# A gated attention block: row sums of squares from x by rows, the last two groups scaled in one pass, and smaller staging

## The chip, the cores and the metric

The kernel runs on one core of one Trainium2 chip. The metric is the device time of one execution in microseconds (us). TensorE is called PE in the profile (PEld is its loading of weights), VectorE DVE, ScalarE ACT, GpSimd POOL, and SyncE, which issues the DMAs here, SP.

## The reference

One layer of a hybrid attention block on x of 2048 x 1024 in float32: an RMS norm, one wide projection, a banded attention (branch A), a sparse attention whose keys are picked by a small index (branch B), a gated merge, an output projection and a second RMS norm.

```python
def rms_norm(x, g):
    y = x * lax.rsqrt(jnp.mean(x * x, axis=-1, keepdims=True) + EPS)
    return y * g
...
xn = rms_norm(h, norm_gain)
proj = xn @ w_in
qa, ka, va, ga, qb, kb, vb, gb, iq, ik, iw, za, zb = jnp.split(proj, offsets, axis=-1)
ya = chunked_relpos_attention(qa, ka, va, rel_bias) * jax.nn.silu(ga)
qb, kb, iq, ik = (partial_rope(z) for z in (qb, kb, iq, ik))
yb = dsa_sparse_attention(qb, kb, vb, iq, ik, iw) * jax.nn.silu(gb)
merged = sigmoid(za + b_merge[0]) * (ya @ w_branch_a) + sigmoid(zb + b_merge[1]) * (yb @ w_branch_b)
h = x + merged @ w_out
out = rms_norm(h, final_norm_gain)
```

The sparse attention scores all earlier keys with relu(iq . ik) weighted by iw, keeps the best 256 per query and attends to these alone.

## The kernel before, in words

**Precision.** Every matmul operand is held as two float32r parts, a rounded high part and the rest, and a product is three matmuls (`mm3`, line 192): high x high, high x low, low x high. A chain is 8 slices k of the model width times 3, that is 24 matmuls into one accumulator of 128 x 512. So each operand needs a split: ScalarE copies the high part, and VectorE or GpSimd subtracts it.

**Order of the work.** The instructions of each engine run in the order in which a list scheduler put them when the program was built; it walks the program in its written order and simulates the engines, so that an instruction whose inputs and buffers are ready can go ahead of one written earlier. On the chip each engine, and SP's queue of DMAs, then goes strictly in that order. A tile with a tag rotates over `bufs` buffers; a new tile waits until the last user of the buffer is done.

**The start (lines 212 to 365).** x is worked on in four groups of 512 rows, in the order 2, 3, 0, 1 (`order`), from `xT`, which holds x transposed (the model width on the partitions). For each group i there are three chains m = 0, 1, 2 (`chain`, line 273) with the weights of the index queries, keys and weights (`load_w`, line 236, staged through tile `wst` of three buffers).
- `split_u` (243) splits x times the norm's gain (`gcol`), not yet divided by the root of its mean square, into xh and xl. There are two slots of xh and xl; groups 2 and 0 share one, 3 and 1 the other.
- `squares` (247): ScalarE squares the eight slices two at a time, GpSimd adds them up. `root_columns` (256): four matmuls with a vector of ones turn the sum into one column per 128 rows; VectorE makes the reciprocal square root in small steps (`rsqrt`, 133), GpSimd spreads it into `rb`. `root_rows` (265): four transposes and a ScalarE copy make of it a row that all partitions hold, `roots_[g]`.
- `evac_i` (281) empties an accumulator: times the roots (286), for m = 0 the rotation with the table `cs` (289 to 293), the split (296, 297), and stores to the scratch tensors iqD, kB and the tile ikT (303 to 308), 24 DMAs a group. `weights_t` (310) transposes the index weights.
- Five accumulators rotate over the 12 chains; two of them (tags acc0 and acc1 of pool `psp`) are also the first two of the main projection.
- `norm` (317) takes groups 0 and 1 a second time: VectorE multiplies x by the roots (322), and x is split again (`split_x`, 206), now scaled. These xh and xl are what the main projection reads first.

**The main projection (line 1144 on).** 20 units of 256 columns (`UNITS`), each for two groups at a time; `prep` (172) loads a unit's weights in pieces of two k through tile `wst` (186), ScalarE copies (188), GpSimd subtracts (189). The first unit's `prep(0)` is written in the start (358); its buffer is the one that x32, the tile with x of the groups 2 and 0, lies in. Between the chains the index logits (`logits`, 408) and the search for the best 256 (`search`, 446) are interleaved by a virtual clock. Halfway, groups 2 and 3 are split again, scaled (`norm_again`, 1133), and the units run once more. When the search is done, `open_early` (699) closes its memory and the attention begins beside the last units of the projection.

**The attention.** For each pair of heads the sums of the softmax are inverted, spread by GpSimd into `rb` (891) or `rbb` (969), transposed and multiplied with the gate (`finish`, 887, and `b_unit`, 959 to 977). Both tiles have the tag `ty`, one buffer, which is also that of the tile `ty` or `tyb`, through which one half of the head's output passes (876, 963).

Of the kernel before, what the change touches and what calls it, by code (L numbers as in the profile page):

```python
# [8 lines left out]
F32 = mybir.dt.float32  # L9
# [12 lines left out]
D = 1024  # L22
# [70 lines left out]
def block_kernel(ctx: ExitStack, tc: tile.TileContext, io, dbg=None):  # L93
# [35 lines left out]
    bm = consts.tile([128, 16], F32, name="bm")  # L129
    nc.sync.dma_start(bm, io["bm"])  # L130
    iw = consts.tile([128, NT, H], F32, name="iw")
# [25 lines left out]
    xpoolr = search_st.enter_context(pool("xTr", side="right"))  # L157
    ikT = xpoolr.tile([128, S], F32R, name="ikT")
# [11 lines left out]
    wcur = {}  # L170

    def prep(u, gate=None):
# [3 lines left out]
        if UNITS[u][0] == "va":  # L176
            st = wpool.tile([128, KT, 32], F32, name="wst", tag="wst", bufs=3)
# [3 lines left out]
        for c in range(2):  # L181
            for k in range(0, KT, 2):
                st = wpool.tile([128, 2, 128], F32, name="wst", tag="wst", bufs=3)
                if gate is not None:
                    nc.gpsimd.tensor_copy(st[:, 0, 0:1], gate)
                nc.sync.dma_start(st, io["wP"][u, c, :, k:k + 2, :])
                hi = wt[:, 0, k:k + 2, c * 128:(c + 1) * 128]
                nc.scalar.activation(hi, st, AF.Copy)  # L188
                nc.gpsimd.tensor_tensor(wt[:, 1, k:k + 2, c * 128:(c + 1) * 128], st, f32(hi), op=OP.subtract)  # L189
# [10 lines left out]
    ones = consts.tile([128, 1], F32, name="ones")  # L200
# [5 lines left out]
    def split_x(s, k, c, src):  # L206

        nc.scalar.activation(xh[s][:, k, c], src, AF.Copy, scale=gcol[:, k:k + 1])
        nc.vector.scalar_tensor_tensor(xl[s][:, k, c], src, gcol[:, k:k + 1], f32(xh[s][:, k, c]),
                                       op0=OP.mult, op1=OP.subtract)  # L210

    with ExitStack() as ph:
# [14 lines left out]
        rb, ra, rt, ssq = work[:, 2], work[:, 3], more[:, 2], more[:, 0:2]  # L227
# [8 lines left out]
        def load_w(m, k):  # L236
            st = wpool.tile([128, 2, 128], F32, name="wst", tag="wst", bufs=3)
# [5 lines left out]
        def split_u(i, c=all_):  # L243
            for k in range(KT):
                split_x(SLOT[order[i]], k, c, x32[i % 2][:, k, c])

        def squares(i):

            for k in range(0, KT, 2):
                sq = ssq if k == 0 else tk.tile([128, 2, 512], F32, name="sq", tag="gt", bufs=2)  # L250
                nc.scalar.activation(sq, x32[i % 2][:, k:k + 2], AF.Square)
                if k:
# [1059 lines left out]
```

## Time and profile before

| what | us |
|---|---|
| median of 3 runs (2237.25 to 2248.39) | 2240.68 |
| the profiled execution | 2252.72 |
| its span | 2250.9 |
| PE busy | 2099.3 |
| DVE busy | 1366.3 |
| ACT busy | 1231.5 |
| POOL busy | 950.8 |

The span is the time from the first to the last instruction of the profiled execution. Line numbers (L197) are those of the kernel before. A row of instructions gives line, engine, operation, output and inputs with their shapes, a count, the busy time and the mean duration in ns, and then the idle time before them and what ended it. A matmul's duration is longer than the distance between two of them, since they are pipelined; a rate is therefore taken from counts in a window.

### The profile page before, as it was taken

The numbers are of one execution on the slowest core, as the hardware profiler recorded it, in microseconds if no ns is written. First come the engines' busy times: TensorE is split into PE (matmuls) and PEld (weight loads), VectorE is DVE, ScalarE is ACT, GpSimd is POOL, SyncE is SP. The second block draws the span as 40 slices with busy tenths as digits, with TensorE's granted clock in tenths as the row PEclk, the third lists the DMA queues.
The fourth block names the chain that finished last, engine by engine and source line by source line (L and its number), as shares of the span: only waits on it lengthen the run. The fifth ranks groups of instructions, "written<-read, shape, count | busy, mean of one in ns | idle before, by whom it ended". The sixth has DMA issues, their size and how long they took to land. (4 is left out here: it accounts for less than half of the span.)

```text
span 2250.9 us, 34069 instructions
## 1 busy us (share of the span) xinstructions
PE 2099.3 (93%) x10890; PEld 1746.5 (78%) x10890; DVE 1366.3 (61%) x3296; ACT 1231.5 (55%) x2508; POOL 950.8 (42%) x1067
## 2 busy tenths in 40 slices
PE   6879999999999999999999888999999999999998
PEld 5667787878878888887977767788778877777786
DVE  7948978678778651012336657667676677664444
ACT  5435656556455552224437657667776678763221
POOL 5536456564463632223315453354333533333420
PEclk9989999999999999999999999999999999999999
DMA  5354344454444332337667553464345631144642
GB/s 195 96 154 125 111 150 130 143 184 132 160 153 138 131 100 100 107 103 235 177 203 228 151 180 114 151 215 153 94 124 167 200 115 38 53 127 131 217 158 85
DMA packets 254650, 322.29 MB, mean 143 GB/s; under 512 B 31744, under 2 KB 156032, under 8 KB 254336
## 3 DMA queue, kind: packets, MB, share of 16 engines
q1 hardware_dynamic: 254464, 320.05, 45.0%
q8 instruction: 87, 1.43, 0.3%
q14 instruction: 99, 0.81, 0.1%
HBM read 213.04 MB, written 105.87 MB: 142 GB/s over the span
## 5 line engine op out<-in xcount | busy, mean ns | idle before, releaser
L197 PE MATMUL acc<-xh,wt 128*128 128x512 f32 x2304 | 741.9, 397 | 6.6 <-ACT wt L188 4.5
L197 PEld LDWEIGHTS acc<-xh,wt 128*128 128x128 f32 x2304 | 434.5, 189 | 106.0 <-ACT wt L188 4.8
L197 PE MATMUL acc<-xl,wt 128*128 128x512 f32 x1152 | 455.0, 395 | 0.0
L189 POOL TENSOR_TENSOR wt<-wst,wt 128x256 fp32r<-128x256 f32 x304 | 241.0, 812 | 349.4 <-ACT wt L188 335.8
L773 POOL TENSOR_TENSOR ptl<-pf,pth 128x512 fp32r<-128x512 f32 (+1 forms) x144 | 179.0, 1243 | 241.9 <-ACT pf L769 204.1
L197 PEld LDWEIGHTS acc<-xl,wt 128*128 128x128 f32 x1152 | 218.0, 189 | 49.6
L776 DVE TENSOR_TENSOR ptl<-pt,pth 128x512 fp32r<-128x512 f32 (+1 forms) x288 | 188.3, 661 | 72.8 <-ACT pth L775 71.1
L436 DVE SCALAR_TENSOR_TENSOR sc<-r,iw,sc 128x512 f32<-128x512 f32 (+2 forms) x190 | 174.5, 937 | 78.5 <-POOL sc L434 47.7
L931 PE MATMUL s<-kBt,qsB 128*128 128x512 f32 (+3 forms) x640 | 192.0, 390 | 10.8 <-DVE mx L752 6.7
L775 ACT ACTIVATE pth<-pt 128x512 fp32r<-128x512 f32 (+1 forms) x288 | 161.6, 578 | 59.8 <-PE pt L948 36.8
L188 ACT ACTIVATE wt<-wst 128x256 fp32r<-128x256 f32 x304 | 115.3, 414 | 135.9 <-DMA wst<-wP 133.6
L428 ACT ACTIVATE r<-lg 128x512 f32<-128x512 f32 (+2 forms) x304 | 152.2, 545 | 67.6 <-DVE sc L436 26.9
L948 PE MATMUL pt<-ident,P 128*128 128x128 f32 x1088 | 171.2, 281 | 8.8 <-DVE sg L896 5.1
L934 ACT ACTIVATE P<-P,mx 128x128 f32<-128x128 f32 (+15 forms) x128 | 154.3, 1207 | 44.2 <-DVE mx L752 43.2
L956 PE MATMUL O<-pth,vBt 128*128 128x256 f32 x544 | 154.8, 300 | 16.7 <-ACT pth L775 7.9
L956 PE MATMUL O<-ptl,vBt 128*128 128x256 f32 x544 | 154.6, 308 | 4.5 <-POOL ptl L773 1.9
L948 PEld LDWEIGHTS pt<-ident,P 128*128 128x128 f32 x1088 | 130.9, 144 | 22.6 <-DVE sg L896 7.7
L752 DVE CUSTOM_DVE_ANT_0 P<-s,mk,mx 128x512 f32<-128x512 f32 (+2 forms) x192 | 125.3, 652 | 31.2 <-PE s L931 23.5
L994 POOL TENSOR_TENSOR dw<-dst,dw 128x512 fp32r<-128x512 f32 x64 | 82.9, 1295 | 129.9 <-ACT dw L993 117.2
L956 PEld LDWEIGHTS O<-pth,vBt 128*128 128x128 f32 x544 | 107.4, 197 | 30.6 <-ACT pth L775 11.5
L931 PEld LDWEIGHTS s<-kBt,qsB 128*128 128x128 f32 x640 | 103.7, 193 | 32.5 <-DVE mx L752 22.5
L956 PEld LDWEIGHTS O<-ptl,vBt 128*128 128x128 f32 x544 | 107.3, 197 | 17.8 <-DVE ptl L776 10.4
(227 smaller groups left out, 4261.9 us busy)
## 6 DMA issues: line engine op xcount, KB each, us to landing
wst<-wP SPq DMA_DIRECT2D x304, 128.0 KB
qs<-qA SPq DMA_DIRECT2D x128, 128.0 KB
kk<-kA SPq DMA_DIRECT2D x56, 256.0 KB
vs<-vA SPq DMA_DIRECT2D x56, 256.0 KB
bias<-biasD SPq DMA_DIRECT2D x32, 320.0 KB
sBD<-ef SPq DMA_DIRECT2D x32, 256.0 KB
sAD<-ef SPq DMA_DIRECT2D x32, 256.0 KB
qsB<-qB SPq DMA_DIRECT2D x16, 512.0 KB
```

The costliest lines, as they stand in the source:

```text
L189: nc.gpsimd.tensor_tensor(wt[:, 1, k:k + 2, c * 128:(c + 1) * 128], st, f32(hi), op=OP.subtract)
L197: nc.tensor.matmul(acc, a, b, start=(i == 0), stop=(i == n - 1))
L428: nc.scalar.activation(r[:, :w], lg[:, :w], AF.Relu)
L436: nc.vector.scalar_tensor_tensor(o_, r[:, :w], wv, o_, op0=OP.mult, op1=OP.add)
L752: nc.vector.tensor_tensor_reduce(dst, ps_, add, 1.0, FMAX if first else mx, OP.add, OP.min, accum_out=mx)
L773: nc.gpsimd.tensor_tensor(lo, pf, f32(hi), op=OP.subtract)
L775: nc.scalar.activation(hi, src, AF.Copy)
L776: nc.vector.tensor_tensor(lo, src, f32(hi), op=OP.subtract)
L931: nc.tensor.matmul(s_ps[:, :w], q[:, h, :], kBt[:, m, a:a + w], start=(m == 0), stop=(m == 1))
L934: nc.scalar.activation(P[:, e, :n], P[:, e, :n], AF.Exp, bias=mx[:, e:e + 1], scale=-1.0, accum_out=st["sum"][:, (u % 2) * 2 + e:(u % 2) * ...
L948: nc.tensor.transpose(pt[:, k, e, :], P[:, e, (kt + k) * 128:(kt + k + 1) * 128], ident)
L956: nc.tensor.matmul(o_, vBt[:, kt + k, :], src[:, k, :], start=(kt + k == 0 and n_ == 0), stop=(kt + k == b and n_ == 1), skip_group_check= ...
```

## The change

- Sums of squares: each group's 512 rows are loaded a second time by rows from `x` (four tiles of 128 x 1024, tag gt, two buffers), and ScalarE squares each and sums along the row. The squares of slices, GpSimd's adds and the matmuls with ones are gone.
- Groups 2 and 3 are treated as before (split unscaled, roots applied when the accumulator is emptied; for m = 0 the table cs is multiplied by the roots on GpSimd instead). Groups 0 and 1 are scaled and split in one pass ahead of their chains: VectorE multiplies by gain and root, ScalarE copies, GpSimd (two of eight slices VectorE) subtracts. Their accumulators are emptied without roots, and `norm` is gone. The roots of groups 0 and 1 are made together.
- The index weights have a staging tile of their own (`wis`, four buffers). The weights of the main projection are staged in pieces of four k through three buffers while the search's memory is open, and in pieces of two through two buffers before and after that.
- `rb` and `rbb` have a buffer of their own (pool `wz`). `bm`, `iw`, `ones` and `flag` move into the search's pool, and `bm` is loaded after the start.

```diff
     def prep(u, gate=None):
...
         for c in range(2):
-            for k in range(0, KT, 2):
-                st = wpool.tile([128, 2, 128], F32, name="wst", tag="wst", bufs=3)
+            pl, n, bufs = stage[-1]
+            for k in range(0, KT, n):
+                st = pl.tile([128, n, 128], F32, name="wst", tag="wst", bufs=bufs)
...
-    def split_x(s, k, c, src):
-
-        nc.scalar.activation(xh[s][:, k, c], src, AF.Copy, scale=gcol[:, k:k + 1])
-        nc.vector.scalar_tensor_tensor(xl[s][:, k, c], src, gcol[:, k:k + 1], f32(xh[s][:, k, c]),
-                                       op0=OP.mult, op1=OP.subtract)
+    def split_x(s, k, src, root, e):
+
+        nc.vector.scalar_tensor_tensor(src, src, gcol[:, k:k + 1], root, op0=OP.mult, op1=OP.mult)
+        nc.scalar.activation(xh[s][:, k], src, AF.Copy)
+        e.tensor_tensor(xl[s][:, k], src, f32(xh[s][:, k]), op=OP.subtract)
...
         def load_w(m, k):
-            st = wpool.tile([128, 2, 128], F32, name="wst", tag="wst", bufs=3)
+            st = xp.tile([128, 2, 128], F32, name="wis", tag="wis", bufs=4)
...
         def squares(i):
-
-            for k in range(0, KT, 2):
-                sq = ssq if k == 0 else tk.tile([128, 2, 512], F32, name="sq", tag="gt", bufs=2)
-                nc.scalar.activation(sq, x32[i % 2][:, k:k + 2], AF.Square)
-                if k:
-                    nc.gpsimd.tensor_tensor(ssq, ssq, sq, op=OP.add)
-            nc.gpsimd.tensor_tensor(ssq[:, 0], ssq[:, 0], ssq[:, 1], op=OP.add)
-
-        def root_columns(i):
-            ss = psl.tile([128, 512], F32, name="ss", tag="lg0")
             for j in range(4):
-                nc.tensor.matmul(ss[:, j:j + 1], ssq[:, 0, j * 128:j * 128 + 128], ones, start=True, stop=True)
-            v = xp.tile([128, 4], F32, name="v4", tag="v4")
-            nc.vector.tensor_scalar(v, ss[:, 0:4], 1.0 / D, EPS, op0=OP.mult, op1=OP.add)
-            r = rsqrt(xp, v, "rs", 4)
-            nc.gpsimd.tensor_copy(rb.rearrange("p (j n) -> p j n", j=4), r[:, :, None].to_broadcast([128, 4, 128]))
+                t = 4 * order[i] + j
+                xr = tk.tile([128, D], F32, name="xrow", tag="gt", bufs=2)
+                nc.sync.dma_start(xr, x[t * 128:(t + 1) * 128, :])
+                nc.scalar.activation(xr, xr, AF.Square, accum_out=ss[:, 4 * i + j:4 * i + j + 1])
+
+        inv_ = {}
+
+        def root_columns(i, n):
+            v = xp.tile([128, 4 * n], F32, name="v4", tag=f"v{n}")
+            nc.vector.tensor_scalar(v, ss[:, 4 * i:4 * i + 4 * n], 1.0 / D, EPS, op0=OP.mult, op1=OP.add)
+            r = rsqrt(xp, v, f"rs{n}", 4 * n)
+            for z in range(n):
+                inv_[i + z] = r[:, 4 * z:4 * z + 4]
 
         def root_rows(i):
+            nc.gpsimd.tensor_copy(rb.rearrange("p (j n) -> p j n", j=4), inv_[i][:, :, None].to_broadcast([128, 4, 128]))
...
             R, acc = roots_[g], accs.pop((i, m))
-            a = ev.tile([128, 512], F32, name="ea", tag="ef")
-            nc.vector.tensor_tensor(a, acc, R, op=OP.mult)
+            src = acc
             if m == 0:
...
-                nc.vector.tensor_tensor(rt[64:128], a[0:64], cs[0:64, 1], op=OP.mult)
-                nc.vector.tensor_tensor(rt[0:64], a[64:128], cs[64:128, 1], op=OP.mult)
-                nc.gpsimd.tensor_tensor(ra, a, cs[:, 0], op=OP.mult)
-                nc.vector.tensor_tensor(ra, ra, rt, op=OP.add)
-                a = aa[i] = ra
+                if i < 2:
+                    nc.gpsimd.tensor_tensor(cs, cs, R[:, None, :].to_broadcast([128, 2, 512]), op=OP.mult)
+                src = aa[i] = ev.tile([128, 512], F32, name="ea", tag="ef")
+                nc.vector.tensor_tensor(src, acc, cs[:, 0], op=OP.mult)
+                nc.vector.tensor_tensor(rt[64:128], acc[0:64], cs[0:64, 1], op=OP.mult)
+                nc.vector.tensor_tensor(rt[0:64], acc[64:128], cs[64:128, 1], op=OP.mult)
+                nc.vector.tensor_tensor(src, src, rt, op=OP.add)
+            elif i < 2:
+                src = more[:, m]
+                nc.vector.tensor_tensor(src, acc, R, op=OP.mult)
...
-            nc.vector.tensor_tensor(e[1], a, f32(e[0]), op=OP.subtract)
+            (nc.gpsimd if m and i < 2 else nc.vector).tensor_tensor(e[1], src, f32(e[0]), op=OP.subtract)
...
-        def norm(i):
-
-            g = order[i]
-            for k in range(0, KT, 2):
-                xn = x32[i % 2][:, k:k + 2]
-                nc.vector.tensor_tensor(xn, xn, roots_[g][:, None, :].to_broadcast([128, 2, 512]), op=OP.mult)
-                for k_ in (k, k + 1):
-                    split_x(SLOT[g], k_, all_, x32[i % 2][:, k_])
...
-                if m == 0:
-                    root_columns(i)
-                    if i < 3:
-                        split_u(i + 1)
-                        squares(i + 1)
+                if m == 0 and i == 0:
+                    split_u(1)
+                    root_columns(0, 1)
+                    squares(1)
+                elif m == 0 and i < 3:
+                    if i == 1:
+                        squares(2)
+                        squares(3)
+                        root_columns(2, 2)
+                    root_rows(i + 1)
+                    for k in range(KT):
+                        split_x(SLOT[order[i + 1]], k, x32[(i + 1) % 2][:, k], roots_[order[i + 1]],
+                                nc.vector if k % 3 == 2 else nc.gpsimd)
                 elif m == 1:
-                    root_rows(i)
-                    if i:
+                    if i == 0:
+                        root_rows(0)
+                        root_columns(1, 1)
+                        root_rows(1)
+                    else:
                         weights_t(i - 1)
                     if i == 3:
-                        norm(2)
                         prep(0)
...
-        norm(3)
...
+    stage.append((evl, 4, 3))
...
     def open_early():
...
+        stage.pop()
...
+        wz = ph.enter_context(pool("wz", side="right"))
...
-        rb = wy.tile([128, n, 2, HD], F32, name="rb", tag="ty", bufs=TYB)
+        rb = wz.tile([128, n, 2, HD], F32, name="rb", tag="rb", bufs=1)
...
-                rb = wy.tile([128, 4, HD], F32, name="rbb", tag="ty", bufs=TYB)
+                rb = wz.tile([128, 4, HD], F32, name="rbb", tag="rb", bufs=1)
...
         def part(k):
...
-            nc.gpsimd.tensor_tensor(xs, xs, roots[g][:, None, :].to_broadcast([128, 2, 512]), op=OP.mult)
             for z in range(2):
-                split_x(SLOT[g], k + z, slice(0, 512), xs[:, z])
+                split_x(SLOT[g], k + z, xs[:, z], roots[g], nc.gpsimd)
```

More of the change, by code (lines that the diff above doesn't have):

```diff
@@ L157, in block_kernel @@
     xpoolr = search_st.enter_context(pool("xTr", side="right"))
+    bm = xpoolr.tile([128, 16], F32, name="bm")
+    iw = xpoolr.tile([128, NT, H], F32, name="iw")
     ikT = xpoolr.tile([128, S], F32R, name="ikT")
@@ L170, in block_kernel @@
     wcur = {}
+    stage = [(wpool, 2, 2)]
     def prep(u, gate=None):
@@ L176, in prep @@
         if UNITS[u][0] == "va":
-            st = wpool.tile([128, KT, 32], F32, name="wst", tag="wst", bufs=3)
+            st = stage[-1][0].tile([128, KT, 32], F32, name="wst", tag="wst", bufs=stage[-1][2])
             nc.sync.dma_start(st, io["wV"][UNITS[u][1]])
@@ L226, in block_kernel @@
         roots_[0], roots_[1] = work[:, 0], work[:, 1]
-        rb, ra, rt, ssq = work[:, 2], work[:, 3], more[:, 2], more[:, 0:2]
+        rb, rt = work[:, 2], work[:, 3]
+        ss = xp.tile([128, 16], F32, name="ss")
         def w_of(m):
@@ L243, in split_u @@
         def split_u(i, c=all_):
+            s, src = SLOT[order[i]], x32[i % 2]
             for k in range(KT):
-                split_x(SLOT[order[i]], k, c, x32[i % 2][:, k, c])
+                nc.scalar.activation(xh[s][:, k, c], src[:, k, c], AF.Copy, scale=gcol[:, k:k + 1])
+                nc.vector.scalar_tensor_tensor(xl[s][:, k, c], src[:, k, c], gcol[:, k:k + 1], f32(xh[s][:, k, c]),
+                                               op0=OP.mult, op1=OP.subtract)
         def squares(i):
-            for k in range(0, KT, 2):
-                sq = ssq if k == 0 else tk.tile([128, 2, 512], F32, name="sq", tag="gt", bufs=2)
-                nc.scalar.activation(sq, x32[i % 2][:, k:k + 2], AF.Square)
-                if k:
-                    nc.gpsimd.tensor_tensor(ssq, ssq, sq, op=OP.add)
-            nc.gpsimd.tensor_tensor(ssq[:, 0], ssq[:, 0], ssq[:, 1], op=OP.add)
-        def root_columns(i):
-            ss = psl.tile([128, 512], F32, name="ss", tag="lg0")
-            for j in range(4):
-                nc.tensor.matmul(ss[:, j:j + 1], ssq[:, 0, j * 128:j * 128 + 128], ones, start=True, stop=True)
-            v = xp.tile([128, 4], F32, name="v4", tag="v4")
-            nc.vector.tensor_scalar(v, ss[:, 0:4], 1.0 / D, EPS, op0=OP.mult, op1=OP.add)
-            r = rsqrt(xp, v, "rs", 4)
-            nc.gpsimd.tensor_copy(rb.rearrange("p (j n) -> p j n", j=4), r[:, :, None].to_broadcast([128, 4, 128]))
+            for j in range(4):
+                t = 4 * order[i] + j
[9 more added lines that the diff above has]
+                inv_[i + z] = r[:, 4 * z:4 * z + 4]
         def root_rows(i):
+            nc.gpsimd.tensor_copy(rb.rearrange("p (j n) -> p j n", j=4), inv_[i][:, :, None].to_broadcast([128, 4, 128]))
             tr = psl.tile([128, 512], F32, name="trr", tag="lg1")
@@ L531, in search_again @@
         nc.tensor.matmul(total, bad[:, NT:NT + 1], ones, start=True, stop=True)
-        flag = consts.tile([128, 1], I32, name="flag")
+        flag = xpoolr.tile([128, 1], I32, name="flag")
         nc.vector.tensor_scalar(flag[0:1], total, 0.5, None, op0=OP.is_gt)
```

18 lines of the change are left out of this document (8 added, 10 removed).

## The prediction

> **What bounds the kernel now.** I read the page first (engines, slices), then the windows of 50 us, then TensorE's waits by stage, and last the timelines of the one stage in which TensorE stands still for long.
>
> ```profile
> span 2250.9 us, 34069 instructions
> PE 2099.3 (93%) x10890; PEld 1746.5 (78%) x10890; DVE 1366.3 (61%) x3296; ACT 1231.5 (55%) x2508; POOL 950.8 (42%) x1067
> 48.86:54.79 5.93, 1.45 (x10) 0.97 (x8) 5.93 (x8) 2.37 (x3) 2.00 (x2) 0.79 0.00 0
> 96.00:120.33 24.33, 11.35 (x50) 8.70 (x50) 19.24 (x34) 10.20 (x22) 9.08 (x11) 0.80 0.45 127
> 120.33:135.56 15.23, 8.47 (x28) 6.31 (x29) 13.11 (x16) 6.55 (x12) 4.32 (x4) 0.72 0.47 144
> 900.00:950.00 50.00, 50.00 (x217) 40.51 (x217) 0.00 (x0) 12.83 (x28) 14.86 (x21) 1.00 0.30 98
> 54.70:106.00 51.30, 44.07 (x168) 33.52 (x168) 0.92 0.31 89
> ```
>
> The window rows give length, then the busy time of PE, PEld, DVE, ACT and POOL with counts, the granted clock, the DMA share and GB/s (the last row, of line 197 alone, has only PE and PEld). TensorE carries the kernel: 93% of the span. In the steady stretch it starts 217 matmuls of 128x512 in 50 us, 0.230 us each; a chain of 24 is 5.5 us. The index chains of the start are 12 x 24 matmuls, 66 us at that rate, and 168 of them (7 chains) start after 54.70. The first row of the main projection starts at 120.33. So the start is where time lies idle:
>
> ```profile
> PE lg L426 <- ACT r L428: 16.6, 15, 2.2
> 48.86 0.40 PE L197 MATMUL xa<-xh,w 128*128 128x512 f32 x1
> 54.79 0.79 PE L197 MATMUL xa<-xh,w 128*128 128x512 f32 x1 [2.75 <-DVE ea L286]
> 105.22 0.39 PE L197 MATMUL xa<-xh,w 128*128 128x512 f32 x1
> 117.12 1.12 PE L268 MATMUL trr<-ident,work 128*128 128x128 f32 x4 [9.03 <-POOL work L263]
> 120.33 0.77 PE L197 MATMUL acc<-xh,wt 128*128 128x512 f32 x1 [2.10 <-DVE ea L286]
> 123.89 0.69 PE L197 MATMUL acc<-xh,wt 128*128 128x512 f32 x2
> 135.56 0.79 PE L197 MATMUL acc<-xh,wt 128*128 128x512 f32 x1 [4.46 <-ACT wt L188]
> ```
>
> The first row is the largest wait of TensorE from 145 to 1000 us (total, times, longest); the others are its timeline (start, us, and in brackets the idle time and what ended it). Three holes are seen. 48.86 to 54.79: no accumulator is free, since line 286, which empties one, waits for the roots of the first group. 105.6 to 120.33: the index chains are done, but the first accumulator of the main projection is one of theirs, and it is released by line 286 only when the last group's roots have come through the transposes of 117.12. Then 24 main matmuls and 4 of the logits (some 6.2 us of work) before TensorE stands again for weight pieces until 135.56. At the restarts the clock is down (0.79, 0.72 in the window rows): from 120.33 to 123.89 eight matmuls start, where 0.230 us each would be 1.9 us, so a restart costs 1.7 us. Counted back, the main projection runs as if it had begun without a stop at 135.56 + 1.7 - 6.2 = 131. From there TensorE is busy almost throughout, so what the start gives up should move the end one for one.
>
> **Part by part: the sums of squares and the roots.** What is removed, from the rows:
>
> ```profile
> L253 POOL TENSOR_TENSOR more<-more,sq 128x1024 f32<-128x1024 f32 x12 | 32.6, 2720 | 15.8 <-ACT sq L251 15.6
> L251 ACT ACTIVATE sq<-x x6: 1040/1057/1062, 24.1 to 77.7; 128x1024 f32<-128x1024 f32 x6
> L1231 ACT ACTIVATION_READ_ACCUMULATOR xr<-hh x32: 184/186/187, 2059.5 to 2243.9; 128x1 f32 x32
> L322 DVE TENSOR_TENSOR x<-x,work x4: 1212/1213/1970, 120.1 to 124.3; 128x1024 f32<-128x1024 f32 x4
> 66.28 3.58 POOL L253 TENSOR_TENSOR more<-more,sq 128x1024 f32<-128x1024 f32 x1 [4.58 <-ACT sq L251]
> 67.52 2.90 DVE L209 SCALAR_TENSOR_TENSOR xl<-x,gcol,xh 128x512 fp32r<-128x512 f32 x1
> L209 DVE SCALAR_TENSOR_TENSOR xl<-x,gcol,xh x24: 736/744/2897, 21.6 to 132.8; 128x512 fp32r<-128x512 f32 x24
> ```
>
> GpSimd loses twelve adds, 32.6 us, and line 254; TensorE loses the column sums. ScalarE keeps 16 squares, now of 128 rows each and with a sum read out: 16 x (1.05 + 0.19) = 19.8 us. VectorE loses the second pass over the last two groups: 8 x 1.21 (line 322) and 16 splits of 0.74, about 21 us, of which four subtractions come back. It also loses the contention: a split of 0.74 us took 2.90 us while GpSimd's add ran. The first hole should thus go: line 286 waited behind eight such stretched splits and late roots. The six chains of groups 2 and 3 then end at 48.86 + 5.5, less 1 us of column sums and 0.4 us for the load of bm taken off the queue's head: 53.
>
> What is added is a new condition: chains of the last two groups need x already scaled, so they wait for their own roots, and these come in one pass (`root_columns(2, 2)`) after all 16 row tiles. Call t the time when the last row tile is squared. After it:
>
> ```profile
> 37.18 0.16 DVE L261 TENSOR_SCALAR v<-ss 128x4 f32<-128x4 f32 x1 [5.06 <-PE ss L259]
> 42.96 0.61 POOL L263 COPY work<-rsy 128x512 f32<-128x512 f32 x1 [1.27 <-DVE rsy L147]
> 76.14 0.60 ACT L269 ACTIVATE roots<-trr 128x512 f32<-128x512 f32 x1 [1.66 <-PE trr L268]
> L773 POOL TENSOR_TENSOR ptl<-pf,pth 128x512 fp32r<-128x512 f32 (+1 forms) x144 | 179.0, 1243 | 241.9 <-ACT pf L769 204.1
> L296 ACT ACTIVATE eh<-ea 128x512 fp32r<-128x512 f32 x8 | 4.7, 616 | 0.0
> ```
>
> The small operations take 37.18 to 42.96, the copy 0.61, four transposes about 0.6, the evacuation 0.60: 8 us with semaphores. The first scaled split is 0.74 on VectorE, 0.62 on ScalarE, 1.24 on GpSimd: 2.6 us. Six chains are 33 us, the restart at a low clock 1.7, the transposes of roots and index weights 2.4 (four times four, at half of the 1.12 us that four took at the low clock of 117.12). Splitting one group is 8 x 0.74 + 2 x 0.66 on VectorE and 6 x 1.24 on GpSimd, 7.2 and 7.4 us side by side, 14.7 if one blocks the other; three chains that share it are 16.5, so the pacing costs between 0 and 10 us, and I take 2. Emptying the accumulators costs nothing of its own: for the first two groups GpSimd scales the rotation tables (one operation a group, where it had four adds), for the last two VectorE has one operation less per chain, and five accumulators rotate. The main projection needs no roots for its first accumulator any more; 1 us for the evacuation. Its start is t + 8 + 2.6 + 33 + 1.7 + 2.4 + 2 + 1 = t + 51.
>
> How late is t? No row tile is loaded here in the trace of before, so bounds:
>
> ```profile
> 11.35 1.40 SPq L234 DMA_DIRECT2D x<-xT  x2
> 1440.15 3.41 DMA dst<-wA
> 159.00 1.13 SPq L1137 DMA_DIRECT2D xs<-xT  x2
> 167.23 2.39 POOL L1138 TENSOR_TENSOR xs<-xs,roots 128x1024 f32<-128x1024 f32 x1 [3.85 <-DMA xs<-xT]
> GB/s 88 250 298 344 413 406 144 170 183 116 203 36 0 4 73 94 72 108 164 0 0 146 41 72 208 197 99 120 63 174 157 160 73 103 53 60 214 202 247 256
> ```
>
> (The last row is the rate from 0 to 165 us in 40 slices.) The loads of x for the first two groups are issued by 12.75 us; the row tiles follow, two buffers in rotation (tag gt). 256 KB landed in 3.41 us in a quiet spell; 512 KB are 0.63 us more at 413 GB/s: an estimate of 4.0. At the other end, a 512 KB load issued at 159.0 was used at 167.23: at most 8 us. With 0.33 us of issue and 1.24 of square, two buffers give a tile each 2.8 to 4.8 us, and 16 tiles 45 to 77 us: t between 58 and 90. I take the nearer row, 58, and 5 us for sharing with the 4 MB of x of the last groups (10 us at 413 GB/s, half of it in the way): t = 63, since after 25 us the queues ran at half of their rate. So TensorE idles from 53 to about 74, and the main projection starts at 114 instead of 131: **-17 us**. A t of 58 without pacing gives -24; 90 gives +10, with full pacing +18.
>
> A rule speaks against this. The Trainium skill, page "SBUF — State Buffer", section "SBUF: two separate sides", says that VectorE with two SBUF inputs and GpSimd hold their shared port in turn, each for a whole instruction; the trace agrees (2.90 us for 0.74 beside GpSimd's 3.58). By it the pacing is the full 10 us, and the start would win 9, not 17.
>
> **The weights' first unit.** At 130 TensorE waited for pieces whose DMAs stood behind 24 stores:
>
> ```profile
> 112.00 0.84 SPq L303 DMA_DIRECT2D iqD<-eh  x2
> 124.47 0.43 SPq L303 DMA_DIRECT2D kB<-el  x1
> L189 POOL TENSOR_TENSOR wt<-wst,wt 128x256 fp32r<-128x256 f32 x304 | 241.0, 812 | 349.4 <-ACT wt L188 335.8
> L188 ACT ACTIVATE wt<-wst 128x256 fp32r<-128x256 f32 x304 | 115.3, 414 | 135.9 <-DMA wst<-wP 133.6
> ```
>
> A group's stores hold SP's queue for 13 us. The buffer for unit 0 is x32's, free in the new order after the third group's split, 30 us before the chains end; 8 pieces with two buffers should be in, so nothing is charged; if they again stand behind the stores, 0 to 9 us come back (the hole was 9). Later, pieces of four k instead of two: ScalarE 0.62 for 2 x 0.414, GpSimd 1.24 for 2 x 0.81; some 30 us of ScalarE are saved in a stage in which TensorE waited 16.6 us for its Relu. Half-microsecond blocks become longer ones, though: **-1** (-5 to +5). The index weights' four buffers cost nothing: TensorE had other chains.
>
> **Late stage.** The last three units (second va, both ka) are staged through two buffers of 128 KB, where three were: 24 pieces, no wait of TensorE on them before; two in flight at 3.41 + 0.42 + 0.81 us make 8 pieces in 19 us, against 22 us of use. **+1** (0 to +10). `rb` in a buffer of its own:
>
> ```profile
>   DVE y L877: 49.5, 13
>   DVE sgB L976: 14.7, 14
> PE pt L948 <- DVE sg L896: 5.1, 7, 1.7
> ```
>
> GpSimd's copy waited 49.5 us in all for the add that frees ty, and VectorE 14.7 for rbb, but TensorE only 5.1 and a few more on what follows: **-2** (-8, or +4 where the order of work is drawn anew).
>
> `norm_again`: for a pair of k GpSimd's one operation of 2.39 us (line 1138) becomes two subtractions of 1.24, VectorE keeps two operations: beside main matmuls, nothing.
>
> Sum: -17 - 1 + 1 - 2 = -19. Against the profiled execution (2252.72 us, of which 2250.9 span) that is 2233.7; that execution was 12 us above the median of the timed ones, so from the median, 2240.68: 2221.7, **2222 us**.
>
> **The rivals.** (1) The rows come early. ScalarE needs only 20 us for them, and if they land by 45, TensorE hardly waits: main start 45 + 51 = 96, change -35 - 2, **2204**. For it: the queues reached 413 GB/s. Against: two buffers. (2) Given back: t near 76, or full pacing by the shared port together with t = 68 (main start 127): change -4 to -6, **2236**. For it: the 8 us landing at 159, and 12 MB of rows and x in one stretch. From t = 71 on, the change is under 0.5%, which is about what a measurement here can tell from none. (3) Slower: SP's queue is in order, and a row tile waiting for its buffer, or issued behind the 24 stores of the first group, holds the rest; with 13 us of stores added to a t of 82 (4.3 us a tile), t = 95 and the start is 146: +15 - 2, **2254**. It decides from t = 93 upward. For it: pieces stood behind stores at 112 to 124; against it: the queue has nothing to store before the first roots. The later parts doing nothing at all (rb, staging) changes 3 us and no case.
>
> **Chances.** Forecast 0.48 (own range 2211 to 2229), early rows 0.20, given back 0.24, slower 0.08. Faster by over 0.5% is the first two, 0.68; within, 0.24; slower 0.08. The range takes in the early rows' middle and the given-back case up to its edge: 2203 to 2242.
>
> **What would show it.** Right: line 286's wait gone at 49 to 55; a new idle of TensorE of some 20 us before the first chain of the third group, ended by a split (VectorE, GpSimd) that waited for roots; the last row's square near 63; main matmuls without a stop from about 114; GpSimd's column of the start without operations of 2.7 us. Wrong: no such idle (case 1), or squares after 71 with SP's queue waiting on gt (2, 3), or TensorE waits on weights after 1000 us or on the Relu above 20 us.

## The result, and the profile after

| kernel | median us (lowest to highest) | ratio to before, 95% interval |
|---|---|---|
| before | 2243.97 (2237.25 to 2248.39, 4 runs) | |
| after | 2151.19 (2150.08 to 2151.86, 4 runs) | 0.9588 [0.956, 0.9617] |

The change wins 93 us where 19 were forecast, and 2151 lies far below the range (2203 to 2242). The sign was right; the reason was not. The start, from which 17 of the 19 us were to come, became slower. The gain is in the attention, in the edit that was priced at 2 us. One execution of a_dep_d, a kernel of the experiments, took 2528.56 us at a granted clock of 0.746; it is left out of that kernel's times, and since it was the profiled one, no lines of it are shown.

Two spans show it. The profiled executions differ by 102 us (2250.9 to 2148.9), 9 more than the medians, since the one of before was 9 us above its median. The last matmul of the main projection starts at 1159.5 before and at 1171.5 after: 12 us are lost up to there. From it to the end of the span it is 1091.4 before and 977.4 after: 114 us are won. The two lines, before and then after:

```profile
1159.50 0.39 PE L197 MATMUL acc<-xh,wt 128*128 128x512 f32 x1
...
1171.51 0.39 PE L198 MATMUL acc<-xh,wt 128*128 128x512 f32 x1
```

First the page of the kernel after, then its timeline of the start (start, us, engine, line, operation; in brackets the idle time and what ended it).

```profile
span 2148.9 us, 33487 instructions
PE 2038.5 (95%) x10858; PEld 1724.1 (80%) x10858; DVE 1334.1 (62%) x3255; ACT 1200.6 (56%) x2376; POOL 911.5 (42%) x941
```

```profile
14.24 1.93 SPq L257 DMA_DIRECT2D xrow<-x  x2
...
32.08 24.44 SPq L257 DMA_DIRECT2D xrow<-x  x9
...
59.55 1.84 SPq L312 DMA_DIRECT2D iqD<-eh  x2
...
73.78 0.86 SPq L257 DMA_DIRECT2D xrow<-x  x2
...
80.82 0.35 SPq L257 DMA_DIRECT2D xrow<-x  x1
...
85.63 1.06 ACT L258 ACTIVATE xrow<-xrow 128x1024 f32<-128x1024 f32 x1 [0.95 <-DMA xrow<-x]
89.99 1.12 PE L273 MATMUL trr<-ident,work 128*128 128x128 f32 x4 [17.32 <-POOL work L270]
...
93.24 1.22 PE L198 MATMUL xa<-xh,w 128*128 128x512 f32 x2 [0.21 <-ACT xh L210]
...
137.64 0.48 PE L198 MATMUL acc<-xh,wt 128*128 128x512 f32 x1
```

Two row tiles are issued at 14.24, the next nine from 32.08 on, behind the loads of x for the last groups; the nine issues take 24.44 us, most of it waits for a buffer (22.4 us; the row stands further below). When the stores of the first groups begin at 59.55, four tiles are left, and these come among the stores, from 73.78 on. So the last tile is squared at 86.8 (1.06 us from 85.63 on, and 0.19 us to read the sum out), not at 63. TensorE then stands 17.32 us before the transposes of the roots, and the main projection starts at 137.64, against the 131 at which it began in effect before.

Then the windows of the attention, the stretch from that matmul to the end and two pieces of 50 us (length, then busy time of PE, PEld, DVE, ACT and POOL with counts, the granted clock, DMA share, GB/s): before, then after.

```profile
1159.50:2250.90 1091.40, 1007.46 (x5762) 846.28 (x5760) 670.41 (x1816) 664.28 (x1320) 428.93 (x403) 0.97 0.47 145
...
1280.00:1330.00 50.00, 44.33 (x234) 36.51 (x234) 24.85 (x73) 26.89 (x58) 28.19 (x26) 0.93 0.67 212
...
1630.00:1680.00 50.00, 45.49 (x281) 38.74 (x280) 35.22 (x96) 37.79 (x74) 17.93 (x20) 0.94 0.41 122
```

```profile
1171.50:2148.90 977.40, 950.74 (x5762) 826.58 (x5760) 664.61 (x1816) 659.27 (x1320) 429.66 (x403) 0.99 0.52 161
...
1280.00:1330.00 50.00, 49.57 (x307) 43.40 (x306) 34.05 (x99) 35.30 (x75) 32.12 (x29) 1.00 0.73 230
...
1630.00:1680.00 50.00, 50.00 (x309) 43.76 (x307) 31.63 (x77) 32.44 (x59) 21.93 (x20) 1.00 0.61 195
```

The work is the same, 5762 matmuls, so the 114 us can be divided. TensorE's idle time falls from 83.9 us to 26.7: that is 57. Its busy time for the same matmuls falls from 1007.5 to 950.7: that is the other 57. Part of the second half is the granted clock. The mean of 0.97 hides that between 1180 and 2050 us the clock of before drops to 0.50 in twelve spells of some 3 to 7 us, where after has one. One of them, behind a stop of TensorE:

```profile
2020.00:2022.00 2.00, 0.00 (x0) 0.00 (x0) 0.00 (x0) 0.06 (x1) 0.00 (x0) 0.95 0.49 181
...
2024.00:2026.00 2.00, 2.00 (x11) 1.90 (x9) 0.49 (x1) 0.82 (x3) 1.59 (x2) 0.50 0.44 131
```

Added up over windows of 4 us, the part of the clock that was not granted comes to 33 us before and 6.5 after, so an estimate of 26 us of the gain is clock. The rest of the second half, some 31 us, is put down to matmuls that overlap less when they come in smaller groups; it is what is left over, and was not measured by itself.

The Trainium skill, page "TensorE: Matmul & The Clock Gate", section "A second HAM failure mode: psum-queue depth-cycling", tells of another kernel, in which TensorE idles for moments between groups of matmuls while it cycles through PSUM banks, and its clock swings between half and full. The trace agrees: the longest wait of TensorE between 1180 and 2050 us is 2.8 us before, and the clock there swings between 1.00 and 0.50. That the stalls bring on the drops is argued: they go away together, but a stretch of 50 us with more idle time need not have a lower clock (1380 to 1430 before: 6.6 us idle, clock 1.00).

Now the waits (engine and line that waited, what it waited for, total us, times, longest), TensorE's from 1180 to 2050 us and GpSimd's from 1000 to 2150, before and after:

```profile
PE d L197 <- ACT dw L993: 8.5, 7, 2.5
PE O L956 <- ACT pth L775: 7.9, 11, 1.2
PE s L931 <- DVE mx L752: 6.7, 18, 0.8
...
PE pt L856 <- DVE sgB L976: 2.1, 4, 0.5
...
PE pt L948 <- DVE sgB L976: 1.7, 4, 0.5
...
POOL rb L892 <- DVE y L877: 49.5, 13, 12.6
POOL rbb L970 <- DVE yb L966: 41.0, 19, 7.7
```

```profile
PE d L198 <- ACT dw L1006: 3.8, 6, 1.4
...
PE O L969 <- DVE yb L979: 1.5, 4, 0.5
...
POOL rb L905 <- DVE sum L903: 23.0, 9, 10.8
POOL rbb L983 <- DVE sumB L981: 21.1, 14, 4.2
```

Before, GpSimd's copies waited 90 us for the output add (y, yb) that frees the tag ty. After, the add is gone from their waits, and 44 of the 57 us that are left are for the reciprocals that they copy. TensorE had only 8.9 us of waits whose last releaser is the multiply behind these copies (5.1 for sg, shown with the prediction, and 2.1 and 1.7 for sgB), but it waited for some twenty other things besides, and nearly all of these waits shrink or vanish too (pth 7.9, mx 6.7). One finish of branch B shows the changed order, before and then after:

```profile
1546.38 0.38 ACT L964 ACTIVATE tyb<-O 64x256 f32<-64x256 f32 x1
...
1546.85 0.42 DVE L965 TENSOR_TENSOR yb<-O,tyb 64x256 f32<-64x256 f32 x1 [0.28 <-issue]
...
1547.28 0.43 DVE L966 TENSOR_TENSOR yb<-O,tyb 64x256 f32<-64x256 f32 x1
...
1547.84 0.40 POOL L970 COPY rbb<-sumB 128x256 f32<-128x256 f32 x1 [3.66 <-DVE yb L966]
...
1549.43 0.38 PE L973 MATMUL pt<-ident,rbb 128*128 128x128 f32 x2
...
1550.25 0.42 DVE L976 TENSOR_TENSOR sgB<-pt,sgB 128x256 f32<-128x256 f32 x1
```

```profile
1545.42 0.17 DVE L981 RECIPROCAL sumB<-sumB 128x4 f32<-128x4 f32 x1
...
1545.66 0.40 POOL L983 COPY rbb<-sumB 128x256 f32<-128x256 f32 x1 [3.15 <-PE pt L961]
...
1551.34 0.38 PE L986 MATMUL pt<-ident,rbb 128*128 128x128 f32 x2
...
1552.18 0.41 DVE L989 TENSOR_TENSOR sgB<-pt,sgB 128x256 f32<-128x256 f32 x1
...
1554.03 0.38 ACT L976 ACTIVATE tyb<-O 64x256 f32<-64x256 f32 x1
...
1555.32 0.43 DVE L979 TENSOR_TENSOR yb<-O,tyb 64x256 f32<-64x256 f32 x1
```

Before, the chain is strict: head's output, two copies, two adds, GpSimd's copy, transposes, multiply. After, copy, transposes and multiply are over before the output is there. On the average of all 32 finishes of branch B and 16 of A, the copy starts 0.8 and 0.9 us after the last add starts in the kernel before, and 16.1 and 14.5 us ahead of it after.

### The profile page after: what moved, and what is told of

Same layout as the page of the kernel before. It is cut to its first block, busy times and chain, and to the rows that moved or that the text cites. A ratio compares the mean times of both kernels' runs of the same rounds, so it can differ in the third digit from the quotient of the medians.

```text
span 2148.9 us, 33487 instructions
## 1 busy us (share of the span) xinstructions
PE 2038.5 (95%) x10858; PEld 1724.1 (80%) x10858; DVE 1334.1 (62%) x3255; ACT 1200.6 (56%) x2376; POOL 911.5 (42%) x941
## 4 chain that ended last, share of the span: by engine, by line
PE 38%; DMA 6%; ACT 3%; issue 2%; DVE 2%; POOL 2%; SPq 1%; DVEq 0%; ACTq 0%; POOLq 0%
PE d L198 6%; PE po L1221 6%; PE O L969 5%; PE s L944 5%; PE pt L961 4%; PE O L879 3%; PE acc L198 3%; PE pt L869 2%; PE s L834 2%; DMA wst<-wP 1%; DMA mf<-mD 1%; DMA dst<-wB 1%; DVE P L765 1%; DMA dst<-wA 1%; POOL dw L1007 1%
## 5 line engine op out<-in xcount | busy, mean ns | idle before, releaser
L190 POOL TENSOR_TENSOR wt<-wst,wt 128x512 fp32r<-128x512 f32 (+1 forms) x172 | 207.9, 1225 | 350.3 <-ACT wt L189 326.2
L961 PE MATMUL pt<-ident,P 128*128 128x128 f32 x1088 | 166.9, 273 | 1.5 <-DVE ptl L789 0.5
L969 PE MATMUL O<-pth,vBt 128*128 128x256 f32 x544 | 148.2, 290 | 2.1 <-DVE yb L979 1.5
L969 PE MATMUL O<-ptl,vBt 128*128 128x256 f32 x544 | 147.2, 296 | 1.4 <-POOL ptl L786 1.0
L189 ACT ACTIVATE wt<-wst 128x512 fp32r<-128x512 f32 (+1 forms) x172 | 92.8, 577 | 87.2 <-DMA wst<-wP 83.6
L494 ACT ACTIVATE jk<-sc,st 128x640 int8<-128x640 f32 (+6 forms) x49 | 71.3, 1455 | 82.3 <-DVE st L512 68.8
L436 PE MATMUL lg<-ikT,iqT 128*128 128x512 f32 (+2 forms) x304 | 98.3, 379 | 18.6 <-ACT r L438 18.6
```

The source lines that it names most:

```text
L190: nc.gpsimd.tensor_tensor(wt[:, 1, k:k + n, c * 128:(c + 1) * 128], st, f32(hi), op=OP.subtract)
L961: nc.tensor.transpose(pt[:, k, e, :], P[:, e, (kt + k) * 128:(kt + k + 1) * 128], ident)
L969: nc.tensor.matmul(o_, vBt[:, kt + k, :], src[:, k, :], start=(kt + k == 0 and n_ == 0), stop=(kt + k == b and n_ == 1), skip_group_check= ...
```

## The experiments

Each kernel was timed beside before on the same chip. Before took 2249.8, 2248.8, 2246.7 and 2248.2 us on the four chips that were used; the ratios are to be compared.

| kernel | median us (lowest to highest) | ratio, 95% interval |
|---|---|---|
| b_mem | 2263.64 (2260.89 to 2268.08) | 1.0061 [1.0041, 1.0082] |
| b_wz | 2149.33 (2148.16 to 2152.54) | 0.9558 [0.9534, 0.9581] |
| a_ty | 2263.81 (2262.24 to 2271.86) | 1.0076 [1.0046, 1.0105] |
| null_bm | 2253.83 (2245.20 to 2259.97) | 1.0028 [1.0012, 1.0045] |
| a_dep | 2270.60 (2261.98 to 2278.26) | 1.0109 [1.0077, 1.0142] |
| a_rb | 2220.51 (2219.88 to 2223.92) | 0.9879 [0.9852, 0.9907] |
| a_rbb | 2192.37 (2191.06 to 2193.80) | 0.9752 [0.9725, 0.9779] |
| a_ty2 | 2196.63 (2193.64 to 2200.30) | 0.9765 [0.9737, 0.9792] |
| a_dep_d | 2178.74 (2177.85 to 2184.19) | 0.9704 [0.9685, 0.9722] |
| a_d | 2176.25 (2173.73 to 2177.34) | 0.9676 [0.9637, 0.9714] |
| v1 | 2146.88 (2144.31 to 2148.06) | 0.9556 [0.9540, 0.9572] |
| v3 | 2142.96 (2140.89 to 2145.20) | 0.9540 [0.9524, 0.9556] |
| v3b | 2131.91 (2131.07 to 2134.28) | 0.9490 [0.9474, 0.9505] |
| v5 | 2157.50 (2153.83 to 2161.58) | 0.9589 [0.9547, 0.9630] |

The theory after the two traces was that the own buffer for `rb` and `rbb` is the whole gain, because it takes the output add out from in front of the copy. The rivals: another part does it (memory and staging, the new start), or any edit that makes the scheduler write another order.

### Which part it is

b_wz is the kernel before with the own buffer, and with what makes room for it (constants in the search's pool, staging through two buffers). b_mem is the same without the own buffer. a_ty is the kernel after without it.

```diff
 # b_mem: before, with
-    bm = consts.tile([128, 16], F32, name="bm")
+    bm = xpoolr.tile([128, 16], F32, name="bm")
...
-                st = wpool.tile([128, 2, 128], F32, name="wst", tag="wst", bufs=3)
+                st = wpool.tile([128, 2, 128], F32, name="wst", tag="wst", bufs=2)
 # b_wz: b_mem, with
-        rb = wy.tile([128, n, 2, HD], F32, name="rb", tag="ty", bufs=TYB)
+        rb = wz.tile([128, n, 2, HD], F32, name="rb", tag="rb", bufs=1)
...
-                rb = wy.tile([128, 4, HD], F32, name="rbb", tag="ty", bufs=TYB)
+                rb = wz.tile([128, 4, HD], F32, name="rbb", tag="rb", bufs=1)
 # a_ty: after, with these two lines the other way round
 # null_bm: before, with the load of bm written behind the start
```

Of b_wz:

> The kernel before with rb and rbb in a buffer of their own, and the memory that this needs (small constants in the search's pool, weight staging with two buffers of two k instead of three); the start is that of before. Theory 1 (sharing the buffer of ty costs the attention its time): about 2135 to 2150 us, the stage from the last main matmul to the end about 980 us long instead of 1091. Theory 2 (any edit makes the scheduler draw another order, and this one was a lucky draw): anything between 2180 and 2270 us.

Of b_mem:

> The same edit of constants and staging, but rb and rbb still in the buffer of ty. Theory 1: 2235 to 2255 us, like before, the last stage about 1090 us. Theory 2: another draw, tens of us away from before in either direction.

Of a_ty:

> The changed kernel with rb and rbb back in the buffer of ty, all else as changed. Theory 1: the gain is lost and the slower start is left, 2245 to 2265 us. Theory 2: somewhere between 2151 and 2250 us. Rival 3 (the larger staging pieces and the new start did it): stays near 2151 us.

Of null_bm:

> The kernel before with nothing but the load of bm moved from the head of the program to after the start. It takes no work away, but the scheduler draws another order on all engines, so it measures what a redraw alone is worth. Theory 1: within 15 us of before. Theory 2: tens of us.

Measured: the own buffer moves the time from 2263.64 to 2149.33 on the side of before, and from 2263.81 to 2151.19 on the side of after: 114 and 113 us. No other part has a gain: everything else of the change together is a_ty, 1.0076, a loss of 17 us, and b_mem alone has 14 of them. The traces put it where the theory has it: from the last matmul of the main projection to the end it is 1094.6 us in b_mem and 981.2 in b_wz, 1091.1 in a_ty and 977.4 in after. b_mem missed its own forecast of 2235 to 2255, by a loss that lies in the main projection. null_bm, which changes nothing but the place of a load and with it the scheduler's order, costs 0.3%, so this one new order is worth some 6 us, not 100. It is a mild test: between 1180 and 1500 us, 1563 of TensorE's 1695 matmuls of before stand in the same sequence in null_bm, 890 in after.

### Which way the shared tag hurts

The tag couples both ways: the copy waits for the add that reads ty, and the next head's ty waits for the transposes that read rb. a_dep keeps the own buffer and gives back the first way alone: GpSimd copies one column of y into rb ahead of the real copy. It adds 48 small copies and nothing else.

```diff
         rb = wz.tile([128, n, 2, HD], F32, name="rb", tag="rb", bufs=1)
+        nc.gpsimd.tensor_copy(rb[:, 0, 0, 0:1], y[:, 0:1])
...
                 rb = wz.tile([128, 4, HD], F32, name="rbb", tag="rb", bufs=1)
+                nc.gpsimd.tensor_copy(rb[:, 0, 0:1], y[:, 0, 0:1])
```

> The changed kernel, rb and rbb in their own buffer, but GpSimd first copies one column of y into it, so that the copy waits for VectorE's add of the head's output, as it did when both shared the buffer; the adds no longer wait for anything of rb. Theory 1a (the loss was that the spreading of the sums and its transposes could only start after the add): the gain is lost, 2250 to 2270 us. Theory 1b (the loss was that the next head's ty waited for TensorE's transposes of rb): stays at 2151 to 2165 us, the 48 small copies being GpSimd's alone.

Measured: 2270.60, 119 us above after and no better than a_ty. The way from the add to the copy alone brings the whole price back, 1092.2 us from the last matmul of the main projection on. The waits are those of before again, on TensorE (1180 to 2050 us) and on GpSimd (1000 to 2150):

```profile
PE s L945 <- DVE mx L765: 8.8, 17, 1.2
PE pt L962 <- DVE sg L910: 8.3, 9, 1.7
PE O L970 <- ACT pth L788: 8.2, 12, 1.2
...
POOL rbb L984 <- DVE yb L980: 51.8, 25, 6.9
POOL rb L905 <- DVE y L890: 42.6, 12, 11.8
```

### How it divides

a_rb gives the own buffer to branch A's 16 copies alone, a_rbb to branch B's 32. a_ty2 has no pool wz, and two buffers of the tag ty for all.

```diff
 # a_rb: after, with
-                rb = wz.tile([128, 4, HD], F32, name="rbb", tag="rb", bufs=1)
+                rb = wy.tile([128, 4, HD], F32, name="rbb", tag="ty", bufs=TYB)
 # a_rbb: after, with
-        rb = wz.tile([128, n, 2, HD], F32, name="rb", tag="rb", bufs=1)
+        rb = wy.tile([128, n, 2, HD], F32, name="rb", tag="ty", bufs=TYB)
 # a_ty2: after, with both of these, and
-SGB, TYB = 1, 1
+SGB, TYB = 1, 2
```

Of a_rb:

> Own buffer only for branch A's rb (16 copies); branch B's rbb (32) shares ty's buffer as before. If every finish pays alike, a third of the 113 us is kept: about 2225 us. If only branch B's finishes pay, 2264; if only branch A's, 2151.

Of a_rbb:

> Own buffer only for branch B's rbb (32 copies); branch A's rb (16) shares ty's buffer. If every finish pays alike, two thirds are kept: about 2189 us. If only branch B's finishes pay, 2151; if only branch A's, 2264.

Of a_ty2:

> No buffer of their own: rb and rbb are in the tag ty again, but ty has two buffers in rotation, the same memory as in the changed kernel. The copy then waits for the add before the last one, which is long done. Theory 1 in either form: 2148 to 2160 us. If a separate tag is what counts (a rotation that couples the branches still costs): 2180 us or more.

Measured, from a_ty's 2263.81: A's copies bring 43 us (2.7 each), B's 71 us (2.2 each), and the sum, 115, is about the 113 that both bring together. So the two branches pay alike, and neither hides the other's price. Two buffers under the shared tag bring 67 of 113 us, where 2148 to 2160 us were expected if that was enough. What holds back the other 45 is open. It is not a wait of the copy: in a_ty2's trace GpSimd's 48 copies wait 3.0 us in all. They do stand later in its order than after, 3.3 (B) and 2.6 us (A) ahead of the add on the average, not 16.1 and 14.5.

### Why 2 to 3 us a finish, where the transposes take 0.4

The transposes write into `rp`, which takes its place in the rotation of the three accumulators pt in PSUM, the memory that TensorE writes its results to (`next_pt`, line 739 of before) through which the transposed softmax weights of all heads pass. Theory: while rp waits for the add, the copy and the multiply, one of three accumulators is held, and the weights of the heads behind it stand still. Rival: the transposes' place in TensorE's strict order does it, whatever they write to. a_dep_d is a_dep with rp in the accumulator d (of the products with w_branch_a and w_branch_b) once the late part of the attention runs, which is so for 45 of the 48 finishes. a_d has rp there too, but no late copy.

```diff
-        rp = next_pt([128, 512])
+        rp = psd.tile([128, 512], F32, name="rp", tag="d", bufs=1) if late else next_pt([128, 512])
...
-                rp = next_pt([128, 2, 128])
+                rp = psd.tile([128, 2, 128], F32, name="rp", tag="d", bufs=1) if late else next_pt([128, 2, 128])
```

Of a_dep_d:

> The kernel after with the copy made to wait for the output add, as in a_dep (2270.6, 114 us above the kernel after), and beside that the transposes of the reciprocals, while the late part of the attention runs, write to the accumulator with tag d and not to one of the three pt accumulators that carry the transposed weights. Theory 'rotation': the late copy costs so much because the transposes' accumulator has its place in pt's rotation, so that the weights of the next heads stand behind it; then at least half comes back, 2210 or less. Rival 'order on TensorE': the transposes stand in TensorE's strict order and everything behind them waits, whatever accumulator they write to; then little comes back, 2250 to 2275.

Of a_d:

> The kernel after, with the transposes of the reciprocals written to the accumulator with tag d in place of one of the three pt accumulators, and no late copy. Control for a_dep_d (2178.7), which stayed 28 us above the kernel after. If the accumulator d itself costs something when the transposes share it, this run is slower than the kernel after by most of the 28 us, 2165 to 2180. If sharing d is free, it stays within 6 us of 2151, and the 28 us belong to the late copy through another way than pt.

Measured, as a table of two by two (us):

| | copy early | copy after the add |
|---|---|---|
| rp among the three pt | 2151.2 (after) | 2270.6 (a_dep) |
| rp in d | 2176.3 (a_d) | 2178.7 (a_dep_d) |

With rp out of the rotation a late copy costs 2.5 us by the medians (some 6 by the ratios), which the intervals of the ratios don't tell from nothing; with rp in it, 119 us (not 114, as the expectation of a_dep_d has it). The theory holds. Sharing d costs 25 us of its own and might hide as much of a late copy's price, but even the late copy with rp in d is 92 us faster than with rp in pt, so at least three quarters of the price are the rotation's. Some 4 of the 25 us show in TensorE's wait for d in the attention of a_d (3.8 us after):

```profile
PE d L198 <- ACT dw L1006: 8.0, 5, 3.0
```

### The start

v1 has the start of before and all else of after. v3 issues the row tiles from ScalarE's queue instead of SP's, v3b also gives them four buffers (tag iqT beside gt), and v5 is v3b with rp in d.

```diff
 # v3: after, with
-                nc.sync.dma_start(xr, x[t * 128:(t + 1) * 128, :])
+                nc.scalar.dma_start(xr, x[t * 128:(t + 1) * 128, :])
 # v3b: v3, with
-                xr = tk.tile([128, D], F32, name="xrow", tag="gt", bufs=2)
+                xr = tk.tile([128, D], F32, name="xrow", tag=("gt", "iqT")[j % 2], bufs=2)
```

Of v1:

> The start of the kernel before (squares of slices, norm, three chains with unscaled x for every group) with all other parts of the kernel after. If the start of the change is a loss of its own, as the first main matmul at 137.6 against an effective 131 says, the time falls by about 7 us from the kernel after, to 2140 to 2147, ratio 0.953 to 0.956. If the new start is neutral or a gain that is hidden elsewhere, 2151 or above.

Of v3:

> The kernel after, the sixteen row tiles issued from ScalarE's queue in place of SP's, still two buffers. Theory 'queue': the last tile was late (86.6) because the tiles stood in SP's queue behind the loads of x and behind the stores of the first group; then the last square is at 55 to 65, the first main matmul 51 us later at 106 to 116, and the time 2121 to 2131. Rival 'bytes': the tiles are late because 8 MB of rows, 8 MB of x and the weights share the DMA engines; then the last square stays at 80 or later and the time within 6 us of 2151.

Of v3b:

> As v3, with four buffers for the row tiles (the tags gt and iqT in turn). If two buffers still pace the tiles at 2.7 us each once they have their own queue, the last square comes at 45 to 50, the first main matmul near 98, the time 2110 to 2118; if the bytes pace them, nothing more than v3 gives.

Of v5:

> v3b (2131.9) with the transposes in the accumulator d. If the pt accumulators still hold TensorE up in the kernel after, the time falls below 2126; if the own buffer for rb has freed them already, within 6 us of 2132, or slower where d is the one shared.

v1 is 0.9556 [0.9540, 0.9572], b_wz with the same start 0.9558, and after 0.9588 [0.956, 0.9617]: the new start is no gain, and by the medians a loss of 2 to 4 us, at the edge of what the intervals tell. The two lines of v3 that matter, its last square and its first main matmul, and those of v3b:

```profile
78.55 1.06 ACT L258 ACTIVATE xrow<-xrow 128x1024 f32<-128x1024 f32 x1 [2.22 <-DMA xrow<-x]
...
131.34 0.48 PE L198 MATMUL acc<-xh,wt 128*128 128x512 f32 x1
```

```profile
64.39 1.07 ACT L258 ACTIVATE xrow<-xrow 128x1024 f32<-128x1024 f32 x1 [2.13 <-DMA xrow<-x]
...
123.81 0.48 PE L198 MATMUL acc<-xh,wt 128*128 128x512 f32 x1
```

A queue of their own brings the last tile from 86.8 to 79.7 only, so the expectation of the theory "queue" (55 to 65) missed, and of the rival "bytes" the late square (80 or later) about came true, the unmoved time did not. Leaving SP's queue took 7 us off, and the move has a price: TensorE's wait for index weights that ScalarE copies grows from 6.8 us in the first 150 to 12.5 in v3 and 19.0 in v3b. Four buffers bring 14 us more, to 65.6, about where the forecast had it; v3b's own expectation (45 to 50) missed too. Over 20 to 40 us the DMA engines of v3b move 386 GB/s, so bytes may set a floor; no run tests it. The time follows the main start, by more than it moves: 6 us earlier with v3 and 8 us in time, 14 us earlier with v3b and 19 us in time. v3b is the fastest kernel here, 2131.91, ratio 0.949 [0.9474, 0.9505], and better than v1: with a queue of its own and buffers enough the new start is worth having. v5 loses 26 us again, the price of sharing d.

On v3 a rule of the Trainium skill bears, page "Trainium Kernel Development and Optimization", section "Key Constraints": transfers issued from several queues run on the same DMA engines, and a second queue saves issue time alone. No run here separates the issue time that was saved from the place in the queue: the second queue gave 7 us in all, the buffers 14.

## Why the prediction was wrong, point by point

**`rb` in a buffer of its own: -2 (-8 to +4) forecast, -113 measured.** This is the step that failed, and it alone makes the miss. The prediction quoted the right row (GpSimd's copy waiting 49.5 us for the add) and read the price off another one: the 5.1 us that TensorE waited for sg. It took the wait named with the last releaser for all that the late copy cost. What the runs put in its place: rp holds one of three accumulators of a rotation that every head passes, so the delay goes on as waits named after others (pth, mx, ptl, dw): 57 us of idle time on TensorE, and 57 us of longer busy time with it, an estimated 26 of them by the clock. The lower bound of -8 had no reason that excluded more: the 90 us that GpSimd waited in 32 listed waits are nearer to the result than the 9 us of TensorE. The sentence "VectorE 14.7 for rbb" had the chain in view, one step short of asking what the accumulator behind it holds up.

**The start: -17 forecast, +2 to +7 measured** (by v1 and b_wz against after, and by the two traces). The formula held where TensorE stood idle at t: main start = t + 51 gives 137.8 from t = 86.8, and 137.64 was measured; v3 has 79.7 + 51 = 130.7 against 131.34. In v3b it is 7 us short, 116.6 against 123.81: there the chains of the first two groups still ran at t = 65.6, until 69.6. Two of its terms were off and cancelled: from the last square to the first chain 6.5 us passed and not 10.6, and the waits for splits were 5.8, not 2. What failed is t, 63 against 86.8. The pace was right (2.6 to 2.8 us a tile between 41 and 58), but the tiles did not begin at 12.75 and run through: SP's order put two at 14.24 and the rest behind the other loads at 32.08, and four among the stores. The third rival had named this mechanism, for t = 95, with "the queue has nothing to store before the first roots" against it; but its stores begin at 59.55, with four tiles still to be issued. The wait of SP's queue for the row tiles in the kernel after, and the splits:

```profile
SPq L257 <- ACT xrow L258: 22.4, 9, 7.5
```

```profile
L209 DVE SCALAR_TENSOR_TENSOR xw<-xw,gcol,work 128x512 f32<-128x512 f32 x8 | 9.5, 1257 | 2.6 <-ACT work L274 2.6
L209 DVE SCALAR_TENSOR_TENSOR x<-x,gcol,work 128x512 f32<-128x512 f32 x8 | 11.6, 1513 | 0.0
L211 POOL TENSOR_TENSOR xl<-x,xh 128x512 fp32r<-128x512 f32 x6 | 10.2, 1725 | 1.3 <-ACT xh L210 1.3
```

The splits were to take 0.74 us on VectorE and 1.24 on GpSimd; side by side they took 1.26 to 1.51 and 1.73. The rule of the shared port (the Trainium skill, "SBUF — State Buffer", "SBUF: two separate sides") thus spoke true on the stretch; TensorE paid 5.8 of the full 10 us.

**What would show it.** Line 286's wait at 49 to 55 was not gone but moved: TensorE stood 10.4 us, until 56.94, for line 299, which empties the same accumulators, and had 24.8 us on GpSimd's spread roots in the first 150 us; so the six chains ended at 64.9, not at 53, which the late t hid; the idle of some 20 us ahead of the third group's chains came (17.32); main matmuls without a stop came, from 137.6; and "squares after 71 with SP's queue waiting on gt" was the sign that the start was wrong, and it is there.

**The weights' first unit and pieces of four: -1 forecast.** The stop at 130 is gone, as said: after 137.64 TensorE waits 1.17 and 0.17 us for weights where it had waited 4.46. The Relu waits did not shrink (18.6 us by the row of logits after, 16.6 before). In sum nothing that a run here can tell.

**Late staging: +1 (0 to +10).** No run has this alone. b_mem comes nearest, with two buffers for all units of the main projection and the moved constants: 1.0061, that is +14 us. They lie in the main projection, whose last matmul starts at 1171.7 in place of 1159.5, but no weight wait of TensorE appears between 1000 and 1175 us in its trace. What makes them was not separated; null_bm shows that a new order alone can move the time by some 6 us.

**The median.** The steps were made against 2252.72 and moved to a median of 2240.68; the medians of before are 2243.97 to 2249.8, so the forecast would have been 3 to 9 us higher with them, and further off.

Open: each kernel was built with its own order of instructions, so how much of the 113 us was written into the order, and how much is waited at run time, wasn't tried. a_ty2 shows that the order can carry a good part, since it loses 45 us with hardly a wait of its copies. That the fault lies in the rotation was shown by a_dep_d and a_d for both together.

## What to carry to other kernels

When a tile shares a buffer with another that is freed late, don't price it by the wait that TensorE has on the step right behind it: follow what the delayed chain holds on its way (here one of three PSUM accumulators that all heads rotate through), and don't take the listed waits for a bound: even the 90 us that GpSimd's copies waited were less than the 113 that they cost. A test that splits this cleanly is two by two: make the step late by a small false dependency, and take its accumulator out of the rotation. And when transfers are added to an in-order queue, write down where in the queue each one will stand before taking a pace from buffers.

## What was not expected of the hardware

With no wait of TensorE over 2.8 us, the granted clock dropped to 0.50 in twelve spells of some 3 to 7 us between 1180 and 2050 us before, against one after. For the same 5762 matmuls the stalls cost 57 us of idle time, and the whole difference is 114: here a stall cost about twice its listed time, an estimate from this one pair of kernels. At the start of the kernel after, where the waits were long, the granted clock was 0.59 over 50 to 100 us, with TensorE busy for 18.27 us of the 50.
